# The first transfer and an occupied TensorE in the opening microseconds of a two-block transformer kernel

## The chip, the core and the metric

The kernel runs on one core of one Trainium2 chip. The metric is the device time of one execution in microseconds (us); lower is better. Engine names as the profile has them: PE is TensorE (PEld its weight loads), DVE is VectorE, ACT is ScalarE, POOL is GpSimd, SP is SyncE, which issues all transfers here.

## The reference

Two networks run one after the other on 256 tokens of width 1024. The first has two layers with a 256-token context beside the latent tokens; only its opening matters here:

```python
for l in range(DEPTH):
    mod_lat = silu_c @ w_ada[l] + b_ada[l]
    mod_ctx = silu_cc @ w_ada[l] + b_ada[l]
    x, ctx = _layer(x, ctx, mod_lat, mod_ctx, ...)
# in _layer
xn = _rms_norm(x, g_norm) * (1 + sc[:, None]) + sh[:, None]
cn = _rms_norm(ctx, g_norm) * (1 + sc_c) + sh_c
... = _split_proj(xn @ w_in)
... = _split_proj(cn @ w_in)
```

So before the first projection with `w_in` can start, two things must be known: the root mean square of every token (a sum of squares over 1024 features) and, per feature, the scale and shift that come from `silu(c) @ w_ada`. After the two layers comes a second network (block attention, latent attention, two convolutional feed-forward layers) and a last norm; the change doesn't touch it.

## The kernel before

Everything is kept feature-major: the 1024 features are 8 blocks (KT) of 128 partitions, and the 512 tokens (256 latent, 256 context) lie along the free axis. `xc` in device memory is x and ctx side by side, and the SBUF tile `xres` (`x0`) of 128 x 8 x 512 floats, 2 MB, holds it. Products are made in pieces: a weight or activation is split into a rounded high part and a remainder (`wh`/`wl`, `xyh`/`xyl`), and three products are summed.

A scheduler with a simulated timeline sets the order of the instructions on each engine, within limits that the code gives: a hand-written list of steps (`PLAN["start"]`, line 47) and `issue_after` bindings (`after`, line 92), which keep an instruction behind another one. The list begins `s d0 b l0 d1 w0 l1 d2 t0`:

- The sums of squares. `load_x` (line 174, called on line 322) fetches x in four transfers of two feature blocks. `Squares.add` (line 263) squares each block on ACT (lines 265 and 268) and adds on DVE (line 270). The sum over the 128 partitions is a product with a matrix of ones on PE (`columns`, line 257): once for the sum of the first seven blocks (tile `t`, then `sqh` on DVE, line 277), once for the last block alone (then `sqm`, line 281). The power -0.5 on POOL (line 286) gives `rcx`: step `s`.
- `b`: `bcast4` (line 300) spreads `rcx` over the partitions by four transposes with the identity matrix `c_ident`, and ACT copies the result to `tg` (line 407).
- `d0` to `d7`: for each feature block k, the products of `s32` (silu of c, tile `s`) with two 512 KB pieces of `w_ada` into `acc` (line 400). `s32` is made on lines 226 to 228 from `c_cvec`.
- `l0` to `l7` (line 409): the result is copied to `adarows`, transposed, and reduced to scale and shift; `t <- xres, gm, tg` on DVE (line 424) and `xyh` on ACT (line 425), `xyl` on DVE (line 426) are the normed block.
- `w0` to `w3`: the split of a 512 KB piece `st` of `w_in_t1` into `wh` and `wl`. `t0` to `t7` (line 432): the twelve products of block k with it, into the four banks `pv`, `pv`, `sc`, `sc`.

All transfers are issued by SP, in the order of the code: the constants `ident`, `cvec`, `b_ada`, `g_norm` (lines 149 and 213 to 215), then x, then the pieces of `w_ada` and `w_in_t1` that lines 381 to 384 order. A transfer takes one of eight semaphores in turn (`DMAHW0` to `DMAHW7` in the rows below), so the ninth is issued when the first has landed, and so on.

Of the kernel before, what the change touches and what calls it, by code (L numbers as in the profile page):

```python
# [10 lines left out]
F32 = mybir.dt.float32  # L11
# [6 lines left out]
KT = 8  # L18
# [46 lines left out]
def tile_two_blocks(ctx: ExitStack, tc: tile.TileContext, A, out, dbg=None):  # L65
# [11 lines left out]
    def bank(tag):  # L77
        return psum.tile([128, 512], F32, name=tag)

    base = ctx.enter_context(tc.tile_pool(name="base", bufs=1))  # L80
    first = ExitStack()
    consts = base

    def const(name):
        ap = A[name]
        t = consts.tile(list(ap.shape), F32, name="c_" + name)
        nc.sync.dma_start(t, ap)
        return t

    last_mm, last_tr, last_load = [None], [None], [None]  # L90

    def after(ins):
# [2 lines left out]
    def mm(o, lhsT, rhs, start=True, stop=True):  # L95
        last_mm[0] = PE.matmul(o, lhsT, rhs, start=start, stop=stop).ins  # L96

    def load(t, src):
        last_load[0] = nc.sync.dma_start(t, src).ins
# [41 lines left out]
    def fetch(src, pieces, key=None):  # L141
# [4 lines left out]
        assert a == src.shape[-1]  # L146
        return r

    ident = const("ident")

    def transpose(o, i):
# [5 lines left out]
    ones = consts.tile([128, 128], F32, name="ones")  # L157
# [1 line left out]
    nhalf = consts.tile([128, 16], F32, name="nhalf")  # L159
    G.memset(nhalf, -0.5)  # L160
    msk0 = consts.tile([128, 2, 128], F32, name="c_masks")
    consts = first.enter_context(tc.tile_pool(name="consts1", bufs=1, side="right", reuse_waits="tile"))

    def rsqrt_into(dst, ss, mean_scale, eps, tmp):

# [4 lines left out]

    def xtile():
        return consts.tile([128, KT, 512], F32, name="xres")

    def load_x(x):
        for k in range(0, KT, 2):
            load(x[:, k:k + 2, :], A["xc"][:, k:k + 2, :])

    mods = {}

# [44 lines left out]
    with tc.tile_pool(name="ada", bufs=1, side="right", reuse_waits="tile") as sb:  # L224
# [1 line left out]
        S.activation(th, c2, AF.Tanh, scale=0.5)  # L226
        V.scalar_tensor_tensor(th, th, 1.0, c2, op0=OP.add, op1=OP.mult)
        V.tensor_scalar(s32[:, :, 0:2], th, 0.5, None, op0=OP.mult)
    x0 = xtile()

    late = {}
    gsec = base.tile([128, 6, 8], F32, name="c_g_sec")

# [74 lines left out]
    def first_layer(l, ncx, x, rc):  # L308
# [9 lines left out]

        order = [2, 3, 0, 1]
        oorder = order if ncx else [0, 1]  # L320
        if l == 0:
            load_x(x)
        pb = rc
        xnh = xy.tile([128, KT, 512], F32R, name="xyh")
        xnl = xy.tile([128, KT, 512], F32R, name="xyl")
# [638 lines left out]

    xy = first.enter_context(tc.tile_pool(name="xy", bufs=1, side="right", reuse_waits="tile"))
    x, rc = first_layer(0, True, x0, None)
    tap("x1", x)
    rc0, hh1, hl1, rc = first_layer(1, False, x, rc)
    tap("x2", x)


    consts = ctx.enter_context(tc.tile_pool(name="consts2", bufs=1, reuse_waits="tile"))
# [529 lines left out]
```

## Time and profile before

| what | us |
|---|---|
| median of three executions | 1135.23 |
| lowest and highest of them | 1131.77 and 1140.31 |
| the profiled execution | 1135.77 |
| its span, from the first to the last instruction | 1134.0 |

The profiled execution is one more execution, 0.5 us above the median of the three; 1.8 us of it lie outside the span that the trace covers. Times in the rows are counted from the start of the span.

### The profile page before, as it was taken

The numbers are of one execution on the slowest core, as the hardware profiler recorded it, in microseconds if no ns is written. First come the engines' busy times: TensorE is split into PE (matmuls) and PEld (weight loads), VectorE is DVE, ScalarE is ACT, GpSimd is POOL, SyncE is SP. The second block draws the span as 40 slices with busy tenths as digits, with TensorE's granted clock in tenths as the row PEclk, the third lists the DMA queues.
The fourth block names the chain that finished last, engine by engine and source line by source line (L and its number), as shares of the span: only waits on it lengthen the run. The fifth ranks groups of instructions, "written<-read, shape, count | busy, mean of one in ns | idle before, by whom it ended". The sixth has DMA issues, their size and how long they took to land.

```text
span 1134.0 us, 20510 instructions
## 1 busy us (share of the span) xinstructions
PE 1091.0 (96%) x7826; PEld 957.0 (84%) x7826; DVE 748.3 (66%) x1614; ACT 596.7 (53%) x1158; POOL 149.0 (13%) x214
## 2 busy tenths in 40 slices
PE   4999999999999999998999999999999999999997
PEld 3687777777777789887777999999998899999996
DVE  4764563765647867876566777776556777777652
ACT  3437543533425565463456565555447956555441
POOL 1150010011001301001210022220011001222100
PEclk9999999998999999998999999999999999999998
DMA  8724311614741333224442455555555335555561
GB/s 335 253 83 149 131 56 38 223 57 153 271 153 57 111 118 110 76 87 165 146 144 83 142 175 188 186 181 181 174 149 155 125 113 177 189 187 184 176 185 39
DMA packets 52610, 167.32 MB, mean 148 GB/s; under 512 B 6816, under 2 KB 10400, under 8 KB 52512
## 3 DMA queue, kind: packets, MB, share of 16 engines
q1 hardware_dynamic: 52512, 166.01, 44.0%
q8 instruction: 62, 1.02, 0.3%
q14 instruction: 36, 0.29, 0.1%
HBM read 164.41 MB, written 1.05 MB: 146 GB/s over the span
## 4 chain that ended last, share of the span: by engine, by line
PE 44%; issue 6%; ACT 1%; DVE 1%; DMA 0%; POOL 0%; POOLq 0%; DVEq 0%; ACTq 0%
PE acc L96 27%; PE sc L96 13%; PE tr L152 2%; PE pv L96 1%; ACT wh L127 1%; DMA st<-b_w_uv 0%; DVE wl L128 0%; DVE hg L1383 0%; PE tr L96 0%; POOL t L1351 0%; DVE rb L1113 0%; ACT sm L1038 0%; ACT sm L1039 0%; ACT Q L1287 0%; DVE hres L1080 0%
## 5 line engine op out<-in xcount | busy, mean ns | idle before, releaser
L128 DVE TENSOR_TENSOR wl<-st,wh 128x1024 fp32r<-128x1024 f32 (+4 forms) x272 | 315.3, 1162 | 137.5 <-ACT wh L127 132.0
L127 ACT CAST wh<-st 128x1024 fp32r<-128x1024 f32 (+4 forms) x272 | 268.7, 993 | 191.1 <-PE acc L96 116.8
L96 PE MATMUL acc<-xyh,wh 128*128 128x512 f32 (+1 forms) x320 | 109.5, 343 | 2.7 <-ACT xyh L127 2.1
L96 PE MATMUL acc<-xyl,wh 128*128 128x512 f32 (+1 forms) x320 | 108.2, 341 | 1.2 <-DVE xyl L128 1.2
L96 PE MATMUL acc<-xyh,wl 128*128 128x512 f32 (+1 forms) x320 | 108.8, 340 | 0.0
L96 PE MATMUL acc<-wh,xyh 128*128 128x512 f32 (+1 forms) x256 | 96.5, 380 | 6.4 <-DVE rb L1113 4.5
L96 PE MATMUL sc<-hl,wh 128*128 128x256 f32 x352 | 99.0, 281 | 0.0
L96 PE MATMUL sc<-hh,wl 128*128 128x256 f32 x352 | 99.0, 281 | 0.0
L96 PE MATMUL acc<-hl,wh 128*128 128x256 f32 x352 | 99.0, 281 | 0.0
L96 PE MATMUL acc<-ah,wh 128*128 128x256 f32 x352 | 99.0, 281 | 0.0
L96 PE MATMUL acc<-al,wh 128*128 128x256 f32 x352 | 99.0, 281 | 0.0
L96 PE MATMUL acc<-ah,wl 128*128 128x256 f32 x352 | 98.9, 281 | 0.0
L96 PE MATMUL sc<-hh,wh 128*128 128x256 f32 x352 | 98.8, 281 | 0.0
L96 PE MATMUL acc<-hh,wh 128*128 128x256 f32 x352 | 98.8, 281 | 0.0
L96 PE MATMUL acc<-hh,wl 128*128 128x256 f32 x352 | 98.8, 281 | 0.0
L96 PE MATMUL acc<-wh,xyl 128*128 128x512 f32 (+1 forms) x256 | 95.5, 373 | 0.0
L96 PE MATMUL acc<-wl,xyh 128*128 128x512 f32 (+1 forms) x256 | 94.7, 373 | 0.0
L96 PEld LDWEIGHTS acc<-xyh,wh 128*128 128x128 f32 x320 | 60.6, 189 | 10.7 <-ACT xyh L127 3.0
L96 PEld LDWEIGHTS acc<-xyl,wh 128*128 128x128 f32 x320 | 60.4, 189 | 8.2 <-DVE xyl L128 1.7
L96 PEld LDWEIGHTS sc<-hl,wh 128*128 128x128 f32 x352 | 66.4, 189 | 0.0
L96 PEld LDWEIGHTS sc<-hh,wh 128*128 128x128 f32 x352 | 66.4, 189 | 0.0
L96 PEld LDWEIGHTS acc<-hh,wl 128*128 128x128 f32 x352 | 66.4, 189 | 0.0
(465 smaller groups left out, 2565.5 us busy)
## 6 DMA issues: line engine op xcount, KB each, us to landing
st<-w_gu SPq DMA_DIRECT2D x88, 512.0 KB, 3.6
st<-w_dn SPq DMA_DIRECT2D x32, 512.0 KB, 3.5
st<-w_in_t SPq DMA_DIRECT2D x24, 512.0 KB, 4.0
st<-w_in_f SPq DMA_DIRECT2D x24, 512.0 KB, 4.5
st<-a_w_qkv SPq DMA_DIRECT2D x24, 512.0 KB, 4.3
st<-w_ada SPq DMA_DIRECT2D x20, 512.0 KB, 4.2
st<-w_out SPq DMA_DIRECT2D x16, 512.0 KB, 4.2
st<-w_dn SPq DMA_DIRECT2D x16, 384.0 KB, 3.2
```

The source lines that it names most:

```text
L96: last_mm[0] = PE.matmul(o, lhsT, rhs, start=start, stop=stop).ins
L127: S.copy(hi, src)
L128: (lo_eng or V).tensor_tensor(lo, src, hi.bitcast(F32), op=OP.subtract)
L152: last_tr[0] = PE.transpose(o, i, ident[:i.shape[0], :i.shape[0]]).ins
```

## The change

x is allocated in a pool that is opened earlier, and its four transfers are issued as the first of all, so that the four constants follow them. After the lines that make `s32`, 34 products of the 128 x 128 matrix of ones (float32) with itself go to an accumulator bank that nothing reads.

```diff
+    consts1 = first.enter_context(tc.tile_pool(name="consts1", bufs=1, side="right", reuse_waits="tile"))
...
+    x0 = consts1.tile([128, KT, 512], F32, name="xres")
+    for k in range(0, KT, 2):
+        load(x0[:, k:k + 2, :], A["xc"][:, k:k + 2, :])
     ident = const("ident")
...
-    consts = first.enter_context(tc.tile_pool(name="consts1", bufs=1, side="right", reuse_waits="tile"))
+    consts = consts1
...
-    def load_x(x):
-        for k in range(0, KT, 2):
-            load(x[:, k:k + 2, :], A["xc"][:, k:k + 2, :])
...
-    x0 = xtile()
-
+
+    idle = bank("sc")
+    for _ in range(34):
+        mm(idle[:, 0:128], ones, ones)
...
-        if l == 0:
-            load_x(x)
```

The scheduler also moves other instructions. On SP, the first rows before the change, with the semaphores that each transfer waits for (`xres` is x, `c_...` the constants, `wh`, `wl` the first pieces of `w_ada`, `st` the first of `w_in_t1`):

```order
L87 DMA c_ident<-ident 128x128
L87 DMA c_cvec<-cvec 128x16
L87 DMA c_b_ada<-b_ada 128x48
L87 DMA c_g_norm<-g_norm 128x16
L99 DMA xres<-xc 128x1024 x4
L99 DMA wh<-w_ada 128x1024 [waits DMAHW0_49]
L99 DMA wl<-w_ada 128x1024 [waits DMAHW1_49]
L99 DMA st<-w_in_t 128x1024 [waits DMAHW2_49]
L99 DMA wh<-w_ada 128x1024 [waits DMAHW3_49]
```

And the same place of the change:

```order
L100 DMA xres<-xc 128x1024 x4
L87 DMA c_ident<-ident 128x128
L87 DMA c_cvec<-cvec 128x16
L87 DMA c_b_ada<-b_ada 128x48
L87 DMA c_g_norm<-g_norm 128x16
L100 DMA wh<-w_ada 128x1024 [waits DMAHW0_49]
L100 DMA wl<-w_ada 128x1024 [waits DMAHW1_49]
L100 DMA st<-w_in_t 128x1024 [waits DMAHW2_49]
L100 DMA wh<-w_ada 128x1024 [waits DMAHW3_49]
```

x went ahead of the constants, and the first four weight pieces, which waited for the four constants, now wait for the four pieces of x.

On PE, from its first product to the first of `t0`, before (`s` is `s32`; the two rows from `wh` and `wl` into `acc` are one `d` step, and the transposes of `adarows` one `l` step):

```order
L96 MATMUL tr<-ones,t_172 128x2 x4
L96 MATMUL tr<-ones,t_199 128x2 x4
L96 MATMUL acc<-wh,s_86 32x256 x4
L96 MATMUL acc<-wl,s_86 32x256 x4
L96 MATMUL acc<-wh,s_86 32x256 x4
L96 MATMUL acc<-wl,s_86 32x256 x4
L152 MATMUL tr<-c_ident,rcx 128x128 x4
L152 MATMUL tr<-c_ident,adarows 128x128 x2
L96 MATMUL acc<-wh,s_86 32x256 x4
L96 MATMUL acc<-wl,s_86 32x256 x4
L152 MATMUL tr<-c_ident,adarows 128x128 x2
L96 MATMUL pv<-wh,xyh 128x512
```

And now:

```order
L97 MATMUL sc<-ones 128x128 x34
L97 MATMUL tr<-ones,t_207 128x2 x4
L97 MATMUL tr<-ones,t_234 128x2 x4
L97 MATMUL acc<-wh,s_91 32x256 x4
L97 MATMUL acc<-wl,s_91 32x256 x4
L156 MATMUL tr<-c_ident,rcx 128x128 x4
L156 MATMUL tr<-c_ident,adarows 128x128 x2
L97 MATMUL acc<-wh,s_91 32x256 x4
L97 MATMUL acc<-wl,s_91 32x256 x4
L156 MATMUL tr<-c_ident,adarows 128x128 x2
L97 MATMUL acc<-wh,s_91 32x256 x4
L97 MATMUL acc<-wl,s_91 32x256 x4
```

The 34 new products stand in front of everything; `d1` moved from ahead of the transposes of `rcx` to behind them, and `d2` behind `l1`. Then `t0` follows, as before.

On ACT the same stretch reads now (`sil_t` is the first step towards `s32`; before, it stood in front of the first square, and `xyh` stood behind both first copies of `adarows`):

```order
L270 ACTIVATE t_234<-xres 128x512
L226 ACTIVATE sil_t<-c_cvec 128x16
L128 CAST wh<-st 128x1024
L411 COPY adarows<-acc 128x256
L407 COPY tg<-tr 128x512
L425 ACTIVATE xyh<-t_268,mod_87 128x256
L411 COPY adarows<-acc 128x256
L425 ACTIVATE xyh<-t_268,mod_87 128x256
```

`sil_t` moved behind the eight squares, and the copy of the second `adarows` behind the first half of `xyh`. On all engines, the orders differ only up to the projections that follow `t7`; from there on they are the same.

## Rows read from the trace of the kernel before

**Rows 1.** All engines in order of time, 12 to 24 us

```profile
12.38 1.15 ACT L268 ACTIVATE t<-xres 128x512 f32<-128x512 f32 x2 [0.83 <-DMA xres<-xc]
13.04 0.69 DVE L270 TENSOR_TENSOR t<-t,t 128x512 f32<-128x512 f32 x1 [0.49 <-ACT t L268]
...
13.85 1.78 PEld L96 LDWEIGHTS tr<-ones,t 128*128 128x128 f32 x8 [13.85 <-issue]
13.88 1.83 PE L96 MATMUL tr<-ones,t 128*128 128x2 f32 x8 [13.88 <-DVE t L270]
...
16.06 1.84 PE L96 MATMUL tr<-ones,t 128*128 128x2 f32 x8 [0.35 <-DVE sqh L277]
...
17.83 1.08 PE L96 MATMUL acc<-wh,s 128*32 128x256 f32 x8
...
18.61 1.04 POOL L286 TENSOR_TENSOR rcx<-sqm,nhalf 128x4 f32<-128x4 f32 x1 [14.75 <-DVE sqm L281]
18.69 1.08 PE L96 MATMUL acc<-wl,s 128*32 128x256 f32 x8
...
19.83 0.37 ACT L411 COPY adarows<-acc 128x256 f32<-128x256 f32 x1 [2.63 <-PE acc L96]
...
20.39 0.79 PE L96 MATMUL acc<-wl,s 128*32 128x256 f32 x8
...
21.12 0.65 PE L152 MATMUL tr<-c_ident,rcx 128*128 128x128 f32 x4
...
21.92 0.64 PE L96 MATMUL acc<-wh,s 128*32 128x256 f32 x8
...
22.37 0.61 PE L96 MATMUL acc<-wl,s 128*32 128x256 f32 x8
...
22.92 0.44 PE L152 MATMUL tr<-c_ident,adarows 128*128 128x128 f32 x2
...
23.56 0.90 ACT L425 ACTIVATE xyh<-t,mod 128x256 fp32r<-128x256 f32 x2
```

**Rows 2.** PE in order of time: the first product of t0

```profile
24.12 0.50 PE L96 MATMUL pv<-wh,xyh 128*128 128x512 f32 x1 [0.76 <-ACT xyh L425]
```

**Rows 3.** Windows: length; busy PE, PEld, DVE, ACT, POOL; PEclk; DMA share; GB/s

```profile
2.00:3.00 1.00, 0.00 (x0) 0.00 (x0) 0.00 (x0) 0.03 (x2) 0.54 (x4) 1.00 0.31 58
3.00:4.00 1.00, 0.00 (x0) 0.00 (x0) 0.35 (x2) 0.20 (x1) 0.25 (x1) 1.00 0.51 71
...
14.00:17.80 3.80, 3.45 (x16) 3.40 (x16) 0.73 (x2) 1.04 (x1) 0.00 (x0) 1.00 1.02 418
...
30.00:40.00 10.00, 10.00 (x64) 6.14 (x63) 6.02 (x16) 3.83 (x8) 0.85 (x3) 1.00 0.90 323
```

**Rows 4.** SP in order of time: issues of transfers

```profile
0.74 0.39 SPq L87 DMA_DIRECT2D c_ident<-ident  x1
...
2.59 1.85 SPq L99 DMA_DIRECT2D xres<-xc  x4
4.49 0.50 SPq L99 DMA_DIRECT2D wh<-w_ada  x1
...
12.31 0.33 SPq L99 DMA_DIRECT2D st<-w_in_t  x1
...
21.27 0.33 SPq L99 DMA_DIRECT2D hsum<-w_ada  x1
```

**Rows 5.** POOL and ACT in order of time: the matrix of ones, the first square

```profile
0.73 0.20 POOL L158 MEMSET ones<- 128x128 f32 x1 [0.29 <-POOLq L1493]
...
6.02 0.63 ACT L265 ACTIVATE t<-xres 128x512 f32<-128x512 f32 x1 [2.82 <-DMA xres<-xc]
```

**Rows 6.** PE in order of time, 216 to 218 and 334 to 338 us

```profile
216.33 0.66 PE L96 MATMUL pv<-C,qkT 128*128 128x130 f32 x4
216.92 0.49 PE L96 MATMUL sc<-qkT 64*128 64x128 f32 x2
...
334.72 1.05 PE L96 MATMUL tr<-ones,tg 128*128 128x2 f32 x8
```

## The prediction

> **What bounds the kernel now.** I read the opening in order of time on all engines first, then the issues on SP, then windows for the transfers and for what follows. The reader is to see one chain up to the first projection product. The last piece of x lands at 12.31 (the `st` issue that waits for it starts then) [rows 4]; ACT squares the last two blocks from 12.38, DVE adds, and PE starts its first product of the whole kernel at 13.88 [rows 1]. Two rounds of sums over the partitions follow, from 13.88 and from 16.06; POOL's power ends at 18.61 + 1.04 = 19.65. PE could then spread `rcx`, but `d0` and `d1` stand in front of it, so the transposes start at 21.12. `xyh` starts at 23.56 [rows 1] and the first product of `t0` at 24.12 [rows 2]. From there PE hardly stops: in the window 30 to 40 it is busy for 10.00 of 10.00 us [rows 3]. So what counts is by how much `t0` starts earlier: PE is the bound behind it, and a shift of it is carried on.
>
> TensorE works slowly at first. A half step of `d` (8 records) takes 18.69 - 17.83 = 0.86 us, and one at 21.92 takes 22.37 - 21.92 = 0.45. The half step that starts at 20.39 lies between (0.73 to the next start), so the change falls at about 21.0, some 7.1 us after PE's first instruction [rows 1]. That is the lower and the higher of its two levels, 1.2 and 2.4 GHz, by the durations; the column of the granted clock reads 1.00 in the slow stretch too (14 to 17.8) [rows 3], so it doesn't show this. The same form of sum over the partitions takes 1.83 us for 8 records at 13.88 [rows 1] and 1.05 at 334.72 [rows 6].
>
> **The change part by part.**
>
> *x first.* Its issue moves from 2.59 to 0.74 [rows 4], by 1.85 us. The first piece landed at 6.02 at the latest [rows 5], 3.4 us after its issue; I keep these intervals. Then the last piece lands at 12.31 - 1.85 = 10.46, and the sums could start at 13.88 - 1.85 = 12.03. From below: nothing gained, if the transfers' pace and not their start sets the landing (12.31). From above: 2.1 MB at the 418 GB/s of the window 14 to 17.8 is 5.0 us, so that x is there at about 8. I take the shift of 1.85, as the rows move as a whole.
>
> *The constants behind x.* They held the DMA engines for 0.31 us in window 2 to 3 and 0.51 in 3 to 4 [rows 3], together 0.8 us, in which x wasn't moving yet; now they stand between x and the weights. `sil_t` needs `cvec`, which lands near 10.46 + 0.8 = 11.3; the scheduler put `sil_t` behind the eighth square (ends near 12.38 + 1.15 - 1.85 = 11.7), so it holds nothing up. If it came later, the cast of `w0`, the copy of `adarows` on ACT and `sqh` on DVE would queue behind it, microsecond for microsecond.
>
> *The waits of the weights.* The first four weight pieces now wait for the four pieces of x. The first is issued at about 4.2 instead of 4.49, the fourth at about 10.5. At each moment three half-megabyte transfers and more are on their way, so the engines shouldn't run dry. The eight semaphores tell when pieces land: `hsum`, issued at 21.27 [rows 4], waits for the second half of `d2`. All weights start 1.85 earlier but behind 0.8 us of constants: 21.27 - 1.85 + 0.8 = 20.2. With the half step of 0.45 behind it, `t0` can't start before 20.7, as `d2` now stands in front of it.
>
> *The chain with a fast PE.* The two sums shrink by 2 x (1.83 - 1.05) = 1.56. From the start of the sums to the end of the power it was 19.65 - 13.88 = 5.77, and becomes 4.2: 12.03 + 4.2 = 16.25. `d1` is out of the way, so the transposes start there and not 1.47 later. From them to `xyh` it was 23.56 - 21.12 = 2.44: 18.7. Now the copy of the second `adarows` stands behind the first half of `xyh` on ACT: 0.45 + 0.37 [rows 1], then its transposes (0.44), then `d2` (0.9): 20.85. So with PE free at 12.03, `t0` starts at 20.85, next to the landing of the weights, 3.25 earlier than 24.12.
>
> *The 34 products.* They need only `ones`, ready at 0.93 [rows 5], so they start at about 1. They cost nothing up to 12.03; beyond that, each microsecond is one of the chain. A float32 product has two records (four products of a sum are 8), so there are 68. The trace doesn't have this form. At the higher clock the nearest rows are the sums, 1.05 / 8 = 0.13 per record with the same weights, and `pv<-C,qkT`, 130 columns against full weights, (216.92 - 216.33) / 4 = 0.15 [rows 6]. At the lower clock the weight loads alone take 1.78 / 8 = 0.22 [rows 1]; twice 0.15 is 0.30. From below: 68 x 0.13 = 8.8, end at 9.8, if the clock were high at once. From above, 7.1 us low and no overlap of load and product: worked out under the rivals. I take 7.1 us of the lower clock, the only row there is, at 0.25 per record (28 records), then 40 at 0.13 = 5.2: they end at 1 + 7.1 + 5.2 = 13.3. That is 1.25 later than the sums need PE.
>
> The trace shows one rise, 7.1 us after the first instruction [rows 1]. The Trainium skill, "TensorE: Matmul & The Clock Gate", Part 1, says that the moment at which the clock rises differs from run to run, so that one shouldn't fit a kernel to a count of slow products. By that rule 34 products are sometimes too many and sometimes too few; by it the sum would lie anywhere between a gain of 2.0 and one of 3.25, and this trace, with one rise, can't say more.
>
> **The sum.** `t0` at 20.85 + 1.25 = 22.1, against 24.12: a gain of 2.0 us. Later moves of the scheduler lie within the projections, between products that PE does back to back; I cost them at nothing, with up to half a microsecond either way. The profiled execution's 1135.77 less 2.0 is 1133.8 with the 1.8 us outside its span unchanged; it lay 0.5 above the median, so the median goes from 1135.23 to about 1133.2.
>
> **The rivals.**
>
> *The end of the 34 products doesn't matter.* The clock rises sooner than 7.1 us, they are over by 12.0, and the landing of `d2` sets `t0`: 20.7 to 20.85. For it: any rise at 4 us or so gives an end near 12. Against it: the only rise on record took longer. Gain 3.3, time 1131.9.
>
> *They overrun (slower).* PE loads the same weights anew for each record; if the load can't overlap the product before it, a record costs load plus product. By the rows the load is 0.22 at the lower clock. A half step of `d` is four products on a quarter of the array each; if these run side by side, its 0.86 us are two records of 256 columns, 0.43 each, and 128 columns take 0.21 [rows 1]. Load plus product is then 0.43, and 0.215 at the higher clock. Then 7.1 us hold 16.5 records, the other 51.5 take 11.1, and the end is 19.2: 7.2 late, `t0` at 28.0, 3.9 us slower, time 1139.1. It decides from an end of 12.03 + 3.25 = 15.3 on. Against it: elsewhere loads run under products, as the 0.15 per record of `C,qkT` shows, with loads of full weights [rows 6].
>
> *Nothing comes through.* x isn't earlier, since its landing goes by the pace of the transfers, or PE, started earlier, meets the next weights before they land and gives the gain back before 40 us. For it: weights land as late as 21.27 for use at 22.37, so the start is close to the transfers' pace already. Against it: from `t0` on PE has no gap [rows 3] while transfers run ahead of it. Gain 0 to 1, time about 1134.7.
>
> **How the numbers follow.** Forecast 0.5, the early end 0.25, nothing 0.13, the overrun 0.12. The predicted time is the forecast's, 1133.2. The four cases span 1131.9 to 1139.1; the three executions of before lie from 3.5 below to 5.1 above their median, so a median of a few can itself be off by some 3. The range is 1128.5 to 1138.5; what it leaves out is part of the overrun and a stray median. About 1% (11.4 us) is what a measurement of this kernel can tell from no change, and no case here reaches it: all of the chain before `t0` that could go is 3.4 us down to the landing of `d2`. Faster by over 1%: 0.02; within: 0.96; slower by over 1%: 0.02.
>
> **What would show it.** In the changed trace: x issued at 0.7 and its last square near 10.5; the 34 products from 1 us, their records halving in length on the way, their end near 13.3; the two sums at about 1.05 each; the transposes of `rcx` no longer behind `d1`; the first product of `t0` near 22.1; the same distance to the end of the span as before, 1134.0 - 24.12 = 1109.9. It is wrong if the 34 products end after 15.3, if x lands later than 11.5, if PE waits for weights between `t0` and 40 us, or if the distance from `t0` to the end changes by more than a microsecond or two.

## The result: 1127.87 us, below the range of the prediction

| | before | after |
|---|---|---|
| first comparison, median of 7 runs each | 1135.23 | 1127.87 (1124.03 to 1133.59) |
| ratio, with 95% interval | | 0.9939 [0.9916, 0.9962] |
| second comparison, median (23 and 12 runs) | 1135.51 | 1133.25 (1127.37 to 1138.03) |
| ratio, with 95% interval | | 0.9961 [0.9941, 0.9981] |
| profiled execution of the first comparison, span | 1134.0 | 1123.7 |

The first comparison gives 7.4 us, the second, made among the experiments, 2.3 between the medians, with intervals that overlap. Both intervals lie under 1, so a gain is shown; how much of the 7.4 belongs to the change is a question of its own, taken up below.

**The opening.** PE in order of time, in the changed kernel:

```profile
0.99 10.63 PE L97 MATMUL sc<-ones 128*128 128x128 f32 x68 [0.99 <-POOL ones L162]
11.45 0.95 PE L97 MATMUL tr<-ones,t 128*128 128x2 f32 x8
12.75 1.02 PE L97 MATMUL tr<-ones,t 128*128 128x2 f32 x8 [0.34 <-DVE sqh L279]
13.71 1.08 PE L97 MATMUL acc<-wh,s 128*32 128x256 f32 x8
14.56 1.08 PE L97 MATMUL acc<-wl,s 128*32 128x256 f32 x8
15.57 1.11 PE L156 MATMUL tr<-c_ident,rcx 128*128 128x128 f32 x4
...
17.04 0.64 PE L97 MATMUL acc<-wh,s 128*32 128x256 f32 x8
...
20.66 0.50 PE L97 MATMUL pv<-wh,xyh 128*128 128x512 f32 x1
```

The products run from 0.99 to 11.62; the two sums start behind them at 11.45 and take 0.95 and 1.02, where they took 1.83 and 1.84 from 13.88 on [rows 1]. The transposes of `rcx` start at 15.57 (21.12 before). The first product of `t0` is at 20.66, 3.46 us earlier than 24.12 [rows 2].

The issues on SP, against [rows 4]:

```profile
0.74 1.82 SPq L100 DMA_DIRECT2D xres<-xc  x4
...
4.64 0.69 SPq L100 DMA_DIRECT2D wh<-w_ada  x1
5.42 0.53 SPq L100 DMA_DIRECT2D wl<-w_ada  x1
7.85 0.33 SPq L100 DMA_DIRECT2D st<-w_in_t  x1
9.14 0.33 SPq L100 DMA_DIRECT2D wh<-w_ada  x1
...
20.07 0.33 SPq L100 DMA_DIRECT2D hsum<-w_ada  x1
```

By the turn of the eight semaphores the issue at 9.14 waits for x's last piece; in the kernel before that was the one at 12.31. So x is complete 3.17 us earlier, from an issue 1.85 earlier. `hsum` waits for the second half of `d2`, at 20.07 where it was 21.27. That half is what `t0` stands behind in this profile, as the weight loads show:

```profile
20.09 0.16 PEld L97 LDWEIGHTS acc<-wl,s 128*32 128x32 f32 x8 [0.41 <-DMA wl<-w_ada]
20.66 0.19 PEld L97 LDWEIGHTS pv<-wh,xyh 128*128 128x128 f32 x1 [0.41 <-issue]
```

**Behind t0.** The list of steps has `t1 l3 d4 t2`. In the kernel before, PE in order of time shows `d4` cut in two by the transposes of `l3`:

```profile
31.28 0.64 PE L96 MATMUL acc<-kh,s 128*32 128x256 f32 x8
31.73 0.61 PE L96 MATMUL acc<-kl,s 128*32 128x256 f32 x6
32.27 0.44 PE L152 MATMUL tr<-c_ident,adarows 128*128 128x128 f32 x2
32.64 0.62 PE L96 MATMUL acc<-kl,s 128*32 128x256 f32 x2
33.19 0.50 PE L96 MATMUL pv<-wh,xyh 128*128 128x512 f32 x1
```

In the changed kernel the scheduler put them in front:

```profile
27.69 0.38 PE L156 MATMUL tr<-c_ident,adarows 128*128 128x128 f32 x2
28.00 0.64 PE L97 MATMUL acc<-kh,s 128*32 128x256 f32 x8
28.46 0.61 PE L97 MATMUL acc<-kl,s 128*32 128x256 f32 x8
29.00 0.50 PE L97 MATMUL pv<-wh,xyh 128*128 128x512 f32 x1
```

From the end of one projection step to the start of the next it is 33.19 - 31.28 = 1.91 us before and 29.00 - 27.69 = 1.31 after. Three products of the second half (6 records) hold PE for 32.27 - 31.73 = 0.54, four (8 records) for 29.00 - 28.46 = 0.54, and the fourth alone for 33.19 - 32.64 = 0.55. So the four run side by side (of the row at 31.28 four records start within 0.02 us), and one taken out of its group costs as much as the group. Before, `d4`, `d6` and `d7` were cut like this and `d5` in halves; after, only `d6` is, in halves. From `t0` to `t5` it was 47.40 - 24.12 = 23.28 and is 41.80 - 20.66 = 21.14: another 2.14. The four steps hold 1.8 of it (1.91, 1.51, 1.91 and 1.91 us before; 1.31, 1.31, 1.50 and 1.31 after), the joints between steps and projections the rest.

The score products of the first attention, far behind the projections, start at 189.42 before and 183.51 after:

```profile
L96 PE MATMUL sc<-qkT x96: 272/272/579, 189.4 to 462.4; 64*128 64x128 f32 x96
```

```profile
L97 PE MATMUL sc<-qkT x96: 272/272/373, 183.5 to 454.2; 64*128 64x128 f32 x96
```

(Durations in ns, least, median and most, and the first and last start in us.) Up to there the gain is 5.9 us, of which 5.60 stand at `t5`. That is the change's own part in this pair of profiles. The other 4.4 us of the two spans' difference (10.3) come behind it. Windows of before, then of after, with the granted clock third from the end:

```profile
252.00:280.00 28.00, 26.69 (x156) 21.67 (x156) 16.75 (x42) 10.14 (x26) 3.35 (x4) 0.88 0.35 129
504.00:532.00 28.00, 25.40 (x169) 23.05 (x168) 21.17 (x43) 15.99 (x26) 2.48 (x3) 1.00 0.57 187
532.00:560.00 28.00, 26.11 (x110) 21.18 (x111) 14.22 (x23) 9.21 (x11) 8.02 (x5) 0.88 0.33 106
```

```profile
252.00:280.00 28.00, 28.00 (x186) 20.55 (x186) 18.77 (x45) 9.90 (x22) 3.36 (x4) 1.00 0.58 201
504.00:532.00 28.00, 23.72 (x123) 20.06 (x123) 15.75 (x33) 9.44 (x15) 5.00 (x5) 0.94 0.48 157
532.00:560.00 28.00, 27.75 (x137) 22.17 (x136) 16.36 (x28) 13.58 (x22) 7.63 (x4) 1.00 0.46 151
```

A mean of 0.88 over 28 us is 0.12 x 28 / 0.5 = 6.7 us at the lower level. Before had two such falls in its middle, after one of half that length: 13.4 us against 3.4. The 10.0 us between them are 5.0 us of work at half speed, an estimate for a stretch that PE bounds throughout; 4.4 were measured. The kernel's code is the same there, and the falls change from one execution to the next.

### The profile page after: what moved, and what is told of

Same layout as the page of the kernel before. It is cut to its first block, busy times and chain, and to the rows that moved or that the text cites. A ratio compares the mean times of both kernels' runs of the same rounds, so it can differ in the third digit from the quotient of the medians.

```text
span 1123.7 us, 20648 instructions
## 1 busy us (share of the span) xinstructions
PE 1092.8 (97%) x7894; PEld 961.8 (86%) x7894; DVE 748.9 (67%) x1614; ACT 597.0 (53%) x1158; POOL 149.4 (13%) x214
## 3 DMA queue, kind: packets, MB, share of 16 engines
q8 instruction: 62, 1.02, 0.4%
HBM read 164.41 MB, written 1.05 MB: 147 GB/s over the span
## 4 chain that ended last, share of the span: by engine, by line
PE 45%; issue 6%; ACT 1%; DVE 1%; POOL 0%; POOLq 0%; DVEq 0%; ACTq 0%
PE acc L97 28%; PE sc L97 13%; PE tr L156 2%; PE pv L97 1%; ACT wh L128 0%; DVE hg L1383 0%; PE tr L97 0%; DVE wl L129 0%; POOL t L1351 0%; ACT sm L1038 0%; DVE rb L1113 0%; ACT sm L1039 0%; ACT Q L1287 0%; DVE hres L1080 0%; ACT L1038 0%
## 5 line engine op out<-in xcount | busy, mean ns | idle before, releaser
L97 PEld LDWEIGHTS sc<-hh,wl 128*128 128x128 f32 x352 | 66.4, 189 | 0.0
```

## Experiments

Eleven runs were made, ten of them of other kernels. Three moments of the profiled executions tell them apart; the medians are those of 12 runs (6 of the run with the constants on ScalarE), and each ratio is against runs of the kernel before on the same chip (medians 1134.76, 1134.79 and 1135.51; the rows of before and of the first comparison have 7 runs).

| run | t0 | t0 to t5 | t5 | score product | median | ratio, interval |
|---|---|---|---|---|---|---|
| before | 24.12 | 23.28 | 47.40 | 189.4 | 1135.23 | |
| after, first comparison | 20.66 | 21.14 | 41.80 | 183.5 | 1127.87 | 0.9939 [0.9916, 0.9962] |
| x first alone | 21.65 | 24.07 | 45.72 | 187.8 | 1134.74 | 0.9997 [0.9974, 1.0019] |
| products alone | 24.60 | 21.15 | 45.75 | 188.3 | 1131.66 | 0.9971 [0.9948, 0.9994] |
| order alone | 24.12 | 20.88 | 45.00 | 187.0 | 1129.69 | 0.9952 [0.9931, 0.9972] |
| x first, order | 21.73 | 21.66 | 43.39 | 185.4 | 1129.63 | 0.9949 [0.9928, 0.9970] |
| products, order | 21.30 | 21.64 | 42.94 | 185.2 | 1132.33 | 0.9960 [0.9939, 0.9981] |
| after, order | 19.78 | 22.02 | 41.80 | 183.7 | 1130.41 | 0.9965 [0.9945, 0.9986] |
| after, 16 products | 21.52 | 21.15 | 42.67 | 183.4 | 1129.98 | 0.9944 [0.9926, 0.9962] |
| after, 60 products | 25.51 | 25.56 | 51.07 | 193.1 | 1138.48 | 1.0015 [0.9997, 1.0033] |
| after, steps cut | 20.51 | 22.98 | 43.49 | 185.4 | 1134.07 | 0.9976 [0.9959, 0.9993] |
| after, constants on ACT | 21.59 | 22.48 | 44.07 | 185.9 | 1130.69 | 0.9941 [0.9919, 0.9962] |
| after again | 20.88 | 21.66 | 42.54 | 183.3 | 1133.25 | 0.9961 [0.9941, 0.9981] |

**1. x first, without the products.** The loop of 34 products is left out of the changed kernel.

> x first, without the 34 products. Two places are read: the first product of t0 (24.12 before, 20.66 with the whole change) and the first score product sc<-qkT (189.42 before, 183.51 with the whole change). Theory A (the start of t0 carries the gain, by x and by a fast PE, and d steps that the scheduler no longer cuts add about 2): x lands 3.2 earlier as in the whole change, the sums are slow (1.83 each), t0 starts near 22.0; the later d steps are cut by transposes as before, so the score product comes about 2 earlier, not 6, and the time falls by about 2 us. Rival B (x alone does it, the products are idle work): t0 near 20.7 and the score product near 183.5, time as with the whole change.

`t0` came at 21.65, 2.47 us earlier, though both sums ran at the lower clock (1.84 each, from 10.82). But the scheduler left three `d` steps cut, and PE waited among the first ones: 24.07 from `t0` to `t5`. At the score product 1.64 are left, and in the medians nothing.

**2. The products, with x behind the constants.** The loop is added to the kernel before.

> The 34 products alone, x behind the constants as before. Theory A: x lands at 12.3 as before, the sums take 1.0 each from 13.9 on, t0 starts near 22.5 (the second weight piece of d2 lands at 21.3); the scheduler happens to leave the d steps whole here, so the score product comes 3.3 to 4 earlier, near 185.8. Rival B (x alone does it): t0 at 24 and the score product at 189.

The products ended at 10.45, PE idled for 3.48 us, the sums ran slowly (1.27 and 1.84 for 8 records each), and `t0` was no earlier, 24.60:

```profile
0.99 9.46 PE L96 MATMUL sc<-ones 128*128 128x128 f32 x68 [0.99 <-POOL ones L158]
13.93 1.27 PE L96 MATMUL tr<-ones,t 128*128 128x2 f32 x8 [3.48 <-DVE t L274]
```

What it gained (1.65 at `t5`) it gained in the order of the `d` steps, which came out whole.

**3. The order alone.** Kernel before, with the transposes in front of the `d` steps by a rule:

```diff
+BEHIND = ("d3", "d4", "d5", "d6", "d7")
...
-                with after(last_mm[0]):
+                with after(last_mm[0]), after(last_tr[0] if f_ in BEHIND else None):
```

> The kernel before with one rule more: d3 to d7 stand behind the transposes of the l step before them, so that no d step is cut. x and PE's start as before. Theory A: t0 at 24.1 as before; each d step that was cut (d4, d6, d7 between its seventh and eighth product, d5 between its halves) takes 1.3 with the transposes instead of 1.9, 1.5, 1.9 and 1.9, so that the score product comes 2.0 earlier, near 187.4, and the time falls by about 2. Rival C (the order of the d steps is nothing, what was gained behind t0 came from x and PE's clock): score product at 189.4.

`t0` stands at 24.12 as before, `t5` is 2.40 earlier, the score product 2.38. So the order alone gives what the profile of the changed kernel shows behind `t0`.

**4. The order and the change.** The same rule in the changed kernel.

> The whole change with the same rule. Only d6 was cut there, between its halves (1.50 instead of 1.31). Theory A: t0 at 20.7, score product at 183.3, time as with the change within a microsecond. Rival C: the same; told apart only if the score product moves by more than 0.5.

`t0` came at 19.78, but the weights of the next step were not there:

```profile
23.37 0.64 PE L98 MATMUL acc<-wh,s 128*32 128x256 f32 x8 [0.35 <-DMA wh<-w_ada]
24.56 0.64 PE L98 MATMUL acc<-wl,s 128*32 128x256 f32 x8 [0.55 <-DMA wl<-w_ada]
```

`t5` is 41.80 to the hundredth as in after. What the opening wins beyond this is lost again to the stream of the weights: `t1` stands at 25.13 (24.84 in after), and the bound order behind it, 16.67 us to `t5` in place of 16.96, makes up for that. That the two agree to the hundredth is chance.

**5. x first and the order, without the products.**

> x first, no products of ones, and d3 to d7 bound behind l's transposes. Theory (two independent gains): t0 as in the run with x first alone, 21.6 us, and the d steps uncut, so the first score product at 21.65 + 162.9 = 184.6 to 185.5 (before 189.42): 4 to 5 us gained at equal clock, against 5.9 of the whole change. Rival (the gain behind t0 belongs to the products, because TensorE stands at the upper clock there thanks to them): first score product no better than 187.8, as with x first alone.

`t0` at 21.73, `t5` at 43.39, score product at 185.40. Against x first alone the order is worth 2.38 at the score product, the same as in the kernel before: the two gains stand beside each other. To experiment 4, which has the same rule and the 34 products, it is 1.7. Not all of that is the faster sums: 0.8 stands within `t0`, whose products wait for `xyl` here (21.73 to 25.41, 3.68 us, against 2.86 there), and sixteen products, which leave the sums slow, reach 183.4 as well (experiment 7).

**6. The products and the order, x behind the constants.**

> The 34 products and the bound order, with x behind the constants as before. Theory: the products add nothing where x comes late, since TensorE idles some 3 us between their end and the first sums: t0 at 24.1 to 24.6, first score product 187.0 to 187.5, as with the bound order alone (187.04). Rival (the products are worth what they save in the sums): t0 under 23.5 and first score product under 186.4.

The expectation fell: `t0` came at 21.30, not at 24.1. In this execution the products ended later than in experiment 2 (11.51 against 10.45) and x came sooner, so that PE idled 1.10 us and not 3.48, and the sums kept the higher clock (the second took 1.02):

```profile
0.99 10.52 PE L97 MATMUL sc<-ones 128*128 128x128 f32 x68 [0.99 <-POOL ones L159]
12.62 1.05 PE L97 MATMUL tr<-ones,t 128*128 128x2 f32 x8 [1.10 <-DVE t L275]
```

So the products don't need x to be first; they need to end close to the sums, and with x late that is a matter of chance.

**7. Sixteen products.** `range(16)` in the changed kernel.

> The changed kernel with 16 products in place of 34; 32 records at 0.213 us end near 7.8, partly at 0.112: 7.4 to 7.8. TensorE then idles 3 us or more before the sums at 10.9 to 11.1. Theory (the products help only if they reach the sums): sums at the lower clock, 1.84 each, as with x first alone; t0 21.2 to 21.9, first score product 0.8 to 1.5 later than after's 183.51 if the scheduler leaves the d steps uncut. Rival (t0 is set by the weights of d2 alone, so the clock of the sums is worth nothing): t0 at 20.7.

They ended at 6.70. PE idled 4.65 us, the second sum took 1.84, and `t0` came at 21.52, as expected. The score product is no later than after's, against the expectation:

```profile
11.35 1.52 PE L97 MATMUL tr<-ones,t 128*128 128x2 f32 x8 [4.65 <-DVE t L272]
13.21 1.84 PE L97 MATMUL tr<-ones,t 128*128 128x2 f32 x8 [0.35 <-DVE sqh L279]
```

It caught up at 98 us: there after's profiled execution waited 0.89 us for a piece of weights, and this one didn't:

```profile
98.65 1.05 PE L97 MATMUL acc<-st,s 128*32 128x512 f32 x4 [0.89 <-DMA st<-w_ada]
```

The second profile of after doesn't have this wait either, and its score product is at 183.3 with `t5` 0.74 later. Against that profile the sixteen lose 0.64 us at `t0`, 0.13 at `t5` and 0.1 at the score product, and the medians show no loss either. So fewer products make the sums slow, but that 34 are worth more than 16 in the time is not shown.

**8. Sixty products.**

> The changed kernel with 60 products in place of 34: 27 records at 0.213 and 93 at 0.112 end at 17.2. Theory: the sums stand behind them on TensorE's queue, 5.7 us late (17.2 instead of 11.5), at the upper clock; no fall of the clock in the opening; t0 at 24.5 to 26, 4 to 5.5 later than after; the scheduler cuts three d steps again, so another 1 to 1.5 behind t0: first score product 188 to 190, time about that of the kernel before (1133 to 1137). Rival (the work behind the sums has slack and eats the delay, weights and rest being there already): t0 under 23.5, first score product under 186.5.

`t0` came at 25.51, within what was expected: the sums stood behind the products until 15.94, and nothing took up the delay. The rest was worse than expected. The scheduler cut three steps again, and behind two waits the clock fell (the projection product at 25.51 takes 0.79 in place of 0.50):

```profile
23.67 0.44 PE L156 MATMUL tr<-c_ident,adarows 128*128 128x128 f32 x2 [1.74 <-ACT adarows L411]
25.51 0.79 PE L97 MATMUL pv<-wh,xyh 128*128 128x512 f32 x1 [1.40 <-ACT xyh L425]
```

The score product is 9.6 later than after's, and the gain is gone.

**9. The steps cut on purpose.** In the changed kernel, `d4`, `d6` and `d7` get the order that they had before:

```diff
+                k = {"l3": 4, "l5": 6, "l6": 7}.get(f_)
...
+                    with after(t_):
+                        st_d(k, range(7))
+                    with after(t_):
+                        st_l(k - 1, last_mm[0])
+                    with after(last_tr[0]):
+                        st_d(k, range(7, 8))
```

(`t_` is the last product of the step ahead; `st_l` binds its transposes behind the product that it is handed.)

> The changed kernel with the steps d4, d6 and d7 cut on purpose, as they stood in the kernel before: their eighth product behind the transposes of the step l before. Everything ahead of t0 is untouched. Theory (the second part of the gain is the uncut d steps): t0 at 20.7 as in after, but three steps of 1.9 us in place of 1.3 to 1.5, so t5 at 43.3 to 43.7 in place of 41.80 and the first score product at 185.0 to 185.6 in place of 183.51: 1.5 to 2 us given back. Rival (the distance from t0 to t5 shrank for another reason, such as weights that come earlier): t5 at 41.8 to 42.2, first score product at 183.5 to 184.

```profile
27.62 0.64 PE L97 MATMUL acc<-kh,s 128*32 128x256 f32 x8
28.07 0.61 PE L97 MATMUL acc<-kl,s 128*32 128x256 f32 x6
28.61 0.44 PE L156 MATMUL tr<-c_ident,adarows 128*128 128x128 f32 x2
28.98 0.62 PE L97 MATMUL acc<-kl,s 128*32 128x256 f32 x2
29.53 0.50 PE L97 MATMUL pv<-wh,xyh 128*128 128x512 f32 x1
```

`t0` is at 20.51, as in after; the cut step takes 29.53 - 27.62 = 1.91 again, `t5` comes at 43.49 (expected 43.3 to 43.7) and the score product at 185.37 (expected 185.0 to 185.6). Made and unmade, the order is worth 1.9 to 2.4 us.

**10. The constants on ScalarE's queue.**

```diff
-        nc.sync.dma_start(t, ap)
+        q = nc.scalar if name in ("ident", "cvec", "b_ada", "g_norm") else nc.sync
+        q.dma_start(t, ap)
```

> The changed kernel with the four small constants issued by ScalarE, so that SP has x's four pieces and then at once the weights: the first two weight pieces are issued at about 2.6 and 3.1 us in place of 4.64 and 5.42. Theory (t0 of the changed kernel waits for d2's weights, which come in a stream that the transfers keep full): weights earlier by 0 to 1.3 us, x later by as much or less, t0 at 19.7 to 20.7; the d steps as the scheduler then orders them, first score product 182.5 to 183.7. Rival (the constants on SP cost nothing, since x fills the transfers while they are issued): t0 and the score product within 0.3 us of after's 20.66 and 183.51.

Neither theory held. The first weights were issued at 4.75 and 5.12, hardly sooner than 4.64 and 5.42, although SP was free from 2.55 on. It waited 2.2 us for `c_ident`, whose semaphore the first weight piece takes: the turn of the eight semaphores goes over the transfers of both engines, so that the weights still wait for x's pieces and the constants. In this execution the clock was low from 14.2 for 10.2 us, and `t0` came at 21.59. What the constants cost on SP stays open, as the clock was different too; the medians show no loss and no clear gain over after.

**11. The changed kernel once more.**

> The changed kernel once more, for a second profile and more runs. Theory: t0 at 20.4 to 20.9, t5 near 41.8, first score product 182.6 to 183.7; the wait of 0.89 us for a weight piece at 98.65 may or may not come again. Time: 5 to 6 us under the kernel before where both have the same mean clock; the medians 5 to 7.5 apart, as the falls of the clock come. Rival (the 7.4 us of the first comparison are the change's own): medians 7 or more apart again, at equal clock too.

The anchors came again: `t0` at 20.88, score product at 183.3, 6.1 us ahead of before. The products ended at 10.71 this time. The time is 1133.25, and its own granted clock was lower in the mean (0.9887 in these 12 runs against 0.9930 in the first 7; 0.9905 in 93 runs of before).

**What the time does beside.** The runs scatter by 10 us, and the clock accounts for it. Take (1 - mean granted clock) x span as the time lost. Runs of before with 5.6 to 5.7 us lost took 1131.0 to 1132.3, those with 15.9 took 1139.2 to 1141.1. Over all kernels a line through each kernel's runs gives 0.79 us per us lost, with 0.95 us left over. Taken to no loss by it, before is at 1127.2, after at 1121.7 (first comparison) and 1122.3 (second), after with the steps cut at 1123.8, x first with the order at 1123.7, the order alone at 1125.2, x first alone at 1126.6. So with all of the low clock taken out the change is worth 4.9 to 5.5 us. That takes out too much: both profiles of after have a fall of 3.4 us in the opening (0.94 over the first 28 us, where before reads 1.00), 1.7 us lost. It belongs to the kernel as far as two profiles tell, and left in at 0.79 per us it makes the gain 3.6 to 4.2. At the score product, where such a fall counts, the gain is 5.9 and 6.1, give or take a single wait such as that of 0.89 us at 98.65. Together: some 4 to 6 us. Of the medians, after's first seven runs had 3.0 us less lost than before's mean (7.9 against 10.8), worth 2.3, and its next twelve had 2.0 more. (The line isn't used for the runs whose clock was low for long in the opening, where PE waits anyway.)

## Why the prediction was wrong

The prediction said 2.0 us and 1133.2, with 1128.5 as the low end. The change is worth some 4 to 6; the median of the first comparison adds some 2 us of clock to that. The direction, the chances (within 1%) and most of the mechanism held; three terms of the sum were off, and one of them was the step that failed.

- *"Later moves of the scheduler ... I cost them at nothing, with up to half a microsecond either way."* This is the step that failed. They were worth 2.1 us between `t0` and `t5`, shown by doing them alone (2.4) and by undoing them (1.9). The argument was that behind `t0` PE does its products back to back, 10.00 of 10.00 us from 30 to 40 [rows 3], so that moves among them can't matter. A busy PE is not a PE at its peak: the fourth product of a group, cut off from the other three, takes 0.55 us that the page counts as busy. That the orders differ up to the projections behind `t7` was known; what the moves cut and joined was not priced.
- *The distance from `t0` to the end.* The prediction named a change of "more than a microsecond or two" as what would make it wrong. By the profiled executions it went from 1109.9 to 1123.7 - 20.66 = 1103.0: 2.4 of it up to the score product (the order, and what little follows), 4.4 behind it (the clock).
- *The end of the 34 products*, 13.3 predicted, 11.62 measured (10.25 to 11.62 in the seven profiles with 34 of them). At the lower level 23 records stand in the 5.00 us from 1 to 6, 0.22 each, where I took 0.25; at the higher 38 in the 4.00 us from 7 to 11, 0.11 each, where I took 0.13:

```profile
1.00:6.00 5.00, 5.00 (x23) 1.00 0.84 289
7.00:11.00 4.00, 4.00 (x38) 1.00 0.97 300
```

The rise came about 5.8 us after PE's first instruction and not 7.1: 8 records stand from 6 to 7 us, 12 from 7 to 8. So the case that came was nearest to the first rival, an end that doesn't matter (0.25): 3.3 us at `t0` and 20.7 for it, against 3.46 and 20.66. That it is so close is in part luck. The sums could have started at 10.8, when DVE was through, and stood behind the products until 11.45; from there to `t0` the chain took 9.21 us in place of 8.82, with the clock low from 13.7:

```profile
8.52 2.29 DVE L272 TENSOR_TENSOR t<-t,t 128x512 f32<-128x512 f32 x3 [0.85 <-ACT t L270]
```

The overrun by load plus product fell: the 68 loads are busy for 10.44 us within the products' 10.63. An end that late came with 60 products, and near the price that the sum gives for it: 16.11 is 4.1 after 12.03, so `t0` at 24.9; measured 25.51.
- *x's landing.* A shift of 1.85 taken, 3.17 measured, between the value and the upper bound. It differs from profile to profile: by the same issues x was complete at 10.89 to 12.31 in the four with the constants first, at 8.59 to 9.77 in the nine with x first. In the windows 2 to 3 and 3 to 4 the transfers are at 0.90 and 1.01 with x, where they were at 0.31 and 0.51 with the constants [rows 3]. Before, six pieces of weights were issued by 8.07, while x was still on the way; after, three, the third at 7.85. That these held x up before is argued from the issues, and no run separates it.
- *The weights of d2*, 20.2 predicted as the landing, 20.07 measured, and `t0` behind them. This held in the profile, but only just: the second half of `d2` starts 20.10 - 19.52 = 0.58 us behind the first, where 0.45 is enough. In experiment 9, with the same opening, these weights were there at 19.58, and `t0` came 0.15 sooner all the same, behind ACT's copy and the transposes of `l1`. First the lines of after, then of experiment 9:

```profile
19.52 0.64 PE L97 MATMUL acc<-wh,s 128*32 128x256 f32 x8
```

```profile
19.51 0.64 PE L97 MATMUL acc<-wh,s 128*32 128x256 f32 x8
19.58 0.55 SPq L100 DMA_DIRECT2D hsum<-w_ada  x1
19.96 0.61 PE L97 MATMUL acc<-wl,s 128*32 128x256 f32 x8
20.51 0.50 PE L97 MATMUL pv<-wh,xyh 128*128 128x512 f32 x1
```

So chain and weights end within some tenths of each other, and x's extra 1.3 us found both in the way. Nothing done in the opening moved `t5` below 41.80: in experiment 4 the weights of `d3` hold PE, in experiment 10 the clock was low.
- *The sums* at 1.05 each: 0.95 and 1.02. *The transposes in front of `d1`*: at 15.57 against 16.25 worked out, though at the lower clock again (1.11).
- *Nothing comes through*, the third rival, is right about x alone in the time: 1.64 us at the score product and a ratio of 0.9997 [0.9974, 1.0019].

The rule weighed in the prediction, that the moment of the clock's rise differs from run to run (the Trainium skill, "TensorE: Matmul & The Clock Gate", Part 1), is borne out: the same 34 products end anywhere from 10.25 to 11.62 in seven profiles. What a late end costs at `t0` is small and no run separates it: in the first profile nothing, as the weights landed at 20.07; in experiment 9, where the weights were there at 19.58 and the sums stood behind the products too, at most 20.51 - (19.58 + 0.57) = 0.4 us, an estimate with after's 0.57 from that landing to `t0`.

## What to carry to other kernels

When a change moves instructions under a scheduler, compare the order on the bound engine over the whole stretch behind the change and price the groups that it cuts or joins, however busy the engine looks: products that run side by side lose that when something is put between them. Judge a gain of half a per cent at a fixed anchor in the trace close behind the change, and compare times only between runs of the same granted clock. Filler on TensorE speeds the first real products only if it ends close ahead of them: a gap of 1.10 us kept the clock here, gaps of 3.48 and 4.65 didn't. What stands beyond their start is paid in full (60 products: sums 4.49 us later, `t0` 4.85).

## What the runs showed of the hardware beside

- The clock can fall again right behind the filler. In after it was at 0.50 from 13.7 to 17.0, although PE had not been idle for more than 0.4 us at a time since 0.99; what it had done last were two sums of two columns per product. In the second profile the fall came at 18.6 instead, behind idle times of 0.72 and 1.00 us:

```profile
13.70:17.00 3.30, 3.30 (x23) 0.50 1.02 417
```

```profile
18.00:22.00 4.00, 3.53 (x21) 0.57 1.03 410
```

- From 1 to 6 us the column of the granted clock reads 1.00 while the records have the length of the lower level (0.22 us against 0.11 from 7 on); a later fall it does show.
- Among identical programs the mean granted clock ran from 0.986 to 0.997 and moved the time of before between 1130.5 and 1141.1 us.
